# A two-layer hybrid decoder trunk: small products spread further, head norms by ln and exp, gate rows through DRAM, Strassen products summed by product

## The chip, the core and the metric

The kernel runs on one core of a Trainium2 chip. Its engines work side by side: PE (TensorE, matrix products), DVE (VectorE, elementwise), ACT (ScalarE, functions and copies), POOL (GpSimd) and SP (SyncE, which here only issues DMAs). The metric is the device time of one execution in microseconds, a median of several runs.

## The reference, cut to what matters

Two layers over 512 positions and 1024 channels, all in float32. Layer 0 mixes tokens by an RG-LRU, layer 1 by gated linear attention (GLA); each is followed by a gated FFN with 2816 hidden channels.

```python
for i in range(DEPTH):
    mod = (c_act @ ada_w[i] + ada_b[i])[:, None, :]
    sh_m, sc_m, gt_m, sh_f, sc_f, gt_f = jnp.split(mod, 6, axis=-1)
    h = rmsnorm(x, norm_g[i, 0]) * (1.0 + sc_m) + sh_m
    y = rglru_mixer(...) if i % 2 == 0 else gla_mixer(...)
    x = x + gt_m * rmsnorm(y, norm_g[i, 1])
    h = rmsnorm(x, norm_g[i, 2]) * (1.0 + sc_f) + sh_f
    y = conv_ffn(h, ...)          # (gelu(conv(h @ w_up)) * ...) @ w_down
    x = x + gt_f * rmsnorm(y, norm_g[i, 3])
# in gla_mixer, per head: log_alpha = log_sigmoid(z @ w_alpha + b) / 16, chunked attention, then
o = rmsnorm(o, norm_g)            # over the 256 channels of a head
return (o * silu(r)) @ w_out
```

## The kernel before, in words

Weights come in units of 128 x 1024 floats (`load_upto`). A unit lands in a `raw` tile, ACT copies it to a rounded high half in a `w` tile, DVE (or, for some, a DMA that accumulates on POOL's queue) makes the low half. A float32 product is three fast products: high by high, high by low, low by high (`mm3`, `down_t`). Every product goes through line 547, so that line is nearly all of PE.

Stages, in order: the norm of x and the first mixer's projections; its recurrence; its output projection (`mixer_out`, `sublayer_out`); the first FFN; GLA; its output; the second FFN; the last residual (`last_down`). An FFN alternates "up" steps (two projections of 24 products, conv, gelu, split) with Strassen steps of the down projection: of its 22 hidden tiles 18 go in groups of four or two tiles by seven block products (`SGROUPS`, `SPROD`, `strassen`), the last four plainly (`SLAST`, `down_t`). Each Strassen product is added from PSUM to one or two of eight output tiles `y` by DVE: 12 additions for each of two token halves per group.

`sublayer_out` computes the output's four token tiles. `down_pair` makes tiles 0 and 1, `residual` multiplies by the gate row, takes mean squares, the root (`rstd_col`, a power on POOL) and updates x (`xbuf`, resident); `turned` transposes the normed x (line 554) back to channels, and the next stage's first four projections run on token halves while tiles 2 and 3 are finished (`proj_halves`). The gate as a row on all partitions comes from `gate_rows`: ACT and DVE scale the identity by a column, and ones times that on PE gives the row.

In GLA the query and key projections came first, `z` gave the decays by a small product per head (96 rows), and then sixteen chunks of value and output-gate projections (`GLA_CHUNKS`) were interleaved with 36 small items (`diag`, seven `level`s and `inter` per head, `SPREAD` = 15). `attend` makes a head's output; its norm (`rstd_bcast`) was four column sums by ones, a power on POOL (line 475) and four broadcasts by the identity, each of them two instructions in float32, into the bank `nr`.

The order on each engine isn't the order of the code. `Sched` records all operations with a duration, then lists them: on PE and SP by recorded number, on the others by the length of what follows; an operation is placed when its inputs are ready by the planner's own clock and its buffers are free. Each engine then runs its list strictly in that order, so an operation that is later on the chip than planned holds all behind it. Slots: `g` (512 floats, general), `gh` (256), `w`, `raw`, `araw`, seven PSUM banks `mm` and one `nr`.

## Time and profile before

| | |
|---|---|
| median of the runs | 1154.21 us (1153.03 to 1156.69, 3 runs) |
| profiled execution, its own time | 1152.12 us |
| its span | 1150.3 us |
| PE busy | 1118.4 us, 97% |
| DVE, ACT, POOL busy | 84%, 58%, 11% |
| HBM read, mean rate | 219.39 MB, 193 GB/s |
| granted PE clock, mean | 0.997 |

The span is what the trace covers; the time has a little around it. "Busy" is the union of an engine's instructions. A gap in brackets after a row is the idle time ahead of it, and the name behind the arrow is what ended it. In names such as mm<-g,w the output stands left (mm and nr are PSUM banks) and the inputs right; a form 128x512 is partitions by elements.

### The profile page before, as it was taken

The numbers are of one execution on the slowest core, as the hardware profiler recorded it, in microseconds if no ns is written. First come the engines' busy times: TensorE is split into PE (matmuls) and PEld (weight loads), VectorE is DVE, ScalarE is ACT, GpSimd is POOL, SyncE is SP. The second block draws the span as 40 slices with busy tenths as digits, with TensorE's granted clock in tenths as the row PEclk, the third lists the DMA queues.
The fourth block names the chain that finished last, engine by engine and source line by source line (L and its number), as shares of the span: only waits on it lengthen the run. The fifth ranks groups of instructions, "written<-read, shape, count | busy, mean of one in ns | idle before, by whom it ended". The sixth has DMA issues, their size and how long they took to land.

```text
span 1150.3 us, 15016 instructions
## 1 busy us (share of the span) xinstructions
PE 1118.4 (97%) x5361; PEld 928.3 (81%) x5361; DVE 961.9 (84%) x1671; ACT 669.5 (58%) x1051; POOL 124.3 (11%) x148
## 2 busy tenths in 40 slices
PE   8999999999999999999999899999999999999996
PEld 6876778888888888777888788888888888888885
DVE  6989888987889989888878689967877887878986
ACT  5489957655455463466889436448656445453442
POOL 1000011011101101101201201011010101001001
PEclk9999999999999999999999999999999999999998
DMA  9889645789878988873564848624466665768531
GB/s 366 293 290 342 184 138 192 192 230 245 231 201 242 237 252 224 207 213 110 169 174 118 229 147 239 218 74 126 132 159 163 171 184 152 188 173 203 149 106 74
DMA packets 62397, 222.47 MB, mean 193 GB/s; under 512 B 6929, under 2 KB 7569, under 8 KB 62322
## 3 DMA queue, kind: packets, MB, share of 16 engines
q1 hardware_dynamic: 48642, 172.22, 43.4%
q0 software_dynamic: 13680, 49.29, 23.9%
q8 instruction: 42, 0.69, 0.2%
q14 instruction: 33, 0.27, 0.1%
HBM read 219.39 MB, written 2.10 MB: 193 GB/s over the span
## 4 chain that ended last, share of the span: by engine, by line
PE 65%; ACT 12%; DVE 10%; DMA 8%; issue 2%; POOL 1%; SPq 0%; DVEq 0%; ACTq 0%; POOLq 0%
PE mm L547 64%; DMA raw<-in_wall_dram 6%; ACT g L520 6%; DVE g L470 3%; ACT w L527 2%; ACT L520 2%; DVE w L470 2%; DVE g L484 1%; DMA araw<-in_adaT_dram 1%; DVE w L484 1%; ACT w L520 1%; DVE araw L484 1%; POOL sm L475 1%; PE nr L547 1%; ACT g L527 1%
## 5 line engine op out<-in xcount | busy, mean ns | idle before, releaser
L547 PE MATMUL mm<-g,w 128*128 128x512 f32 (+2 forms) x2758 | 614.3, 380 | 0.1
L547 PEld LDWEIGHTS mm<-g,w 128*128 128x128 f32 (+1 forms) x2758 | 501.4, 188 | 99.3 <-issue 1.4
L547 PE MATMUL mm<-w,g 128*128 128x512 f32 (+1 forms) x1428 | 332.8, 389 | 4.0 <-DVE g L470 3.8
L547 PEld LDWEIGHTS mm<-w,g 128*128 128x128 f32 x1428 | 264.9, 188 | 59.6 <-DVE g L470 5.0
L527 ACT CAST w<-raw 128x1024 fp32r<-128x1024 f32 x206 | 212.0, 1038 | 107.1 <-DMA raw<-in_wall_dram 93.4
L470 DVE TENSOR_TENSOR w<-raw,w 128x1024 fp32r<-128x1024 f32 x157 | 188.2, 1208 | 26.7 <-ACT w L527 26.3
L484 DVE SCALAR_TENSOR_TENSOR g<-mm,const,g 128x510 f32<-128x510 f32 (+3 forms) x199 | 146.6, 747 | 55.0 <-ACT g L520 46.0
L470 DVE TENSOR_TENSOR g<-g,g 128x256 f32<-128x256 f32 (+3 forms) x264 | 142.5, 568 | 34.0 <-ACT g L520 23.8
L470 DVE TENSOR_TENSOR g<-g,mm 128x512 f32<-128x512 f32 (+1 forms) x241 | 153.3, 681 | 15.1 <-PE mm L547 13.0
L520 ACT ACTIVATE g<-mm,const 128x512 f32<-128x512 f32 x115 | 86.8, 761 | 83.3 <-PE mm L547 81.1
L520 ACT ACTIVATE g<-g 128x512 f32<-128x512 f32 (+1 forms) x147 | 76.1, 549 | 82.7 <-DVE g L484 60.5
L562 POOL DMA_DIRECT2D w<-in_wall_dram x49 | 42.7, 871 | 506.3 <-ACT w L520 440.7
L484 DVE SCALAR_TENSOR_TENSOR araw<-araw,const 128x1024 f32<-128x1024 f32 x72 | 87.2, 1220 | 11.2 <-DMA araw<-in_adaT_dram 11.2
L547 PE MATMUL mm<-g,g 128*128 128x256 f32 (+3 forms) x508 | 78.4, 309 | 0.2 <-DVE g L470 0.2
L527 ACT CAST g<-g 128x512 fp32r<-128x512 f32 (+1 forms) x80 | 47.3, 602 | 53.2 <-DVE g L470 51.0
L547 PEld LDWEIGHTS mm<-g,g 128*128 128x128 f32 (+1 forms) x508 | 70.4, 191 | 5.7 <-DVE g L470 0.6
L520 ACT ACTIVATE w<-raw 128x1024 fp32r<-128x1024 f32 x49 | 51.8, 1058 | 39.7 <-DMA raw<-in_wall_dram 38.3
L475 POOL TENSOR_TENSOR sm<-sm,const 128x1 f32<-128x1 f32 (+2 forms) x34 | 35.9, 1057 | 283.4 <-DVE sm L484 191.7
L562 POOL DMA_DIRECT2D raw<-in_wall_dram x46 | 40.0, 870 | 208.9 <-DMA raw<-in_wall_dram 65.0
L520 ACT ACTIVATE g<-mm 128x512 f32<-128x512 f32 x44 | 25.9, 595 | 20.7 <-PE mm L547 11.0
L520 ACT ACT_TABLE_LOAD x24 | 30.8, 1283 | 1.1 <-PEq L1669 0.7
L484 DVE SCALAR_TENSOR_TENSOR w<-w,const 128x1024 f32<-128x1024 f32 x24 | 28.9, 1222 | 0.3 <-DMA w<-in_adaT_dram 0.3
(115 smaller groups left out, 716.4 us busy)
## 6 DMA issues: line engine op xcount, KB each, us to landing
raw<-in_wall_dram SPq DMA_DIRECT2D x218, 512.0 KB, 4.7
araw<-in_adaT_dram SPq DMA_DIRECT2D x72, 512.0 KB, 4.9
w<-in_wall_dram POOLq DMA_DIRECT2D x49, 512.0 KB, 8.5
raw<-in_wall_dram POOLq DMA_DIRECT2D x44, 512.0 KB, 7.2
w<-in_adaT_dram SPq DMA_DIRECT2D x24, 512.0 KB, 7.6
const<-in_xT_dram SPq DMA_DIRECT2D x4, 512.0 KB, 5.3
const<-in_x_dram SPq DMA_DIRECT2D x4, 512.0 KB, 10.7
out_dram<-const SPq DMA_DIRECT2D x8, 256.0 KB, 2.0
```

Of the source, the lines that this page charges most:

```text
L470: self.s.add(eng, dur, lambda: e.tensor_tensor(out.ap(), a.ap(), b.ap(), op=op), [a, b], [out])
L475: lambda: self.nc.gpsimd.tensor_tensor(out.ap(), a.ap(), b.ap(), op=ALU.pow), [a, b], [out])
L484: return self.nc.vector.scalar_tensor_tensor(out.ap(), a.ap(), f(sc), b.ap(), op0=op0, op1=op1, **kw)
L520: return self.nc.scalar.activation(out.ap(), a.ap(), func, **kw)
L527: self.s.add("act", (0.095 if self._sb(a) else 0.052) + out.n * 0.8325e-3, lambda: self.nc.scalar.copy(out.ap(), a.ap()), [a], [out], afte ...
L547: r.append(self.nc.tensor.matmul(g[0].ap(), g[1].ap(), g[2].ap(), start=g[3], stop=g[4], **kw))
L562: self.s.add("pool", 1.2, lambda: self.nc.gpsimd.dma_start(out.ap(), src, accum_op=ALU.add), [out], [out], xfer=nbytes / 180e3)
```

## The change

Six edits, with the planner's figures among them.

- GLA: the last five query and key projections become chunks; the 36 small items are spread over chunks 3 to 20 instead of 1 to 15. The last eight columns of the conditioning move into the second FFN.
- Head norm: one column sum onto all partitions by two fast products (`colsum`, after a cast on ACT and a subtraction on DVE), then Ln and Exp with scale -0.5 on ACT. `gated_to` follows when its output gate is there.
- Gate rows: PE transposes the eight columns, ACT copies them, SP stores them to DRAM and loads them back twice, broadcast to all partitions.
- Strassen: each of the seven products of a token half has an accumulator of its own; `outputs` makes the eight `y` tiles once at the end by 16 additions. Four of the seven live in `xbuf`, so x is stored to DRAM after each mixer and read back into `g` tiles (`old`) after the last up step.
- x's first load stands after the recurrence instead of after the first weights.
- Planner: a model of two DMA queues, durations of DVE and ACT times 1.04, a small random offset on priorities, one bank in reserve; slots g 43 to 42, gh 10 to 9, araw 2 to 3.

```diff
+SUMS = ("f0", "f1")
+SOUT = {7: (0, 0), 5: (0, 1), 2: (1, 0), 6: (1, 1)}
-GLA_CHUNKS = ([("v", t) for t in range(4)] + [("r", 0), ("r", 1), ("r", 2), ("r", 3), ("v", 4), ("v", 5),
-              ("v", 6), ("v", 7), ("r", 4), ("r", 5), ("r", 6), ("r", 7)])
-GLA_ENDS = (6, 9, 14, 16)
-SPREAD = 15
+GLA_CHUNKS = ([("q", n) for n in range(4, 9)] + [("v", t) for t in range(4)] + [("r", n) for n in range(4)] +
+              [("v", t) for t in range(4, 8)] + [("r", n) for n in range(4, 8)])
+GLA_ENDS = (11, 14, 18, 20)
+SPREAD = 2, 20
...
-DMA_LAT = 2.0
+DMA_LAT = 2.2
+DMA_HW, DMA_SW = (393e3, 132e3, 1.63, 1.11, 0.34), (220e3, 123.5e3, 1.74, 1.85, 0.0)
+SEEDS, NUDGE = (10, 10, 10, 10, 10, 10), 0.5
+MARGIN = {"dve": 1.04, "act": 1.04}
...
     def gate_rows(layer, part, late):
...
         rows = [gt(), gt()]
+        ps, cols, dr = mmtile(), gtn(P), s.buf("dram", F32, P, KD)
+        o = part * KD
+        s.add("pe", 0.112, lambda: nc.tensor.transpose(ps[0:P].rows(KD).ap(), mod[layer][o:o + KD].ap(), ident[:].ap()),
+              [mod[layer][o:o + KD], ident[:]], [ps[0:P]], after=late)
+        e.acopy(cols.rows(KD), ps[0:P].rows(KD))
+        e.store(dr[:], cols.rows(KD), KD * P * 4)
         for f in range(2):
-            hi, lo = gt(FR), gt(FR)
-            for k in range(4):
-                c = slice(k * P, (k + 1) * P)
-                e.act(hi[c], ident[:], AF.Copy, scale=mcol(layer, part, 4 * f + k), after=late)
-                e.stt(lo[c], ident[:], mcol(layer, part, 4 * f + k), hi[c].f32(), ALU.mult, ALU.subtract)
-            ps = mmtile()
-            e.mms([(ps[:], onesr[:], hi[:], True, False), (ps[:], onesr[:], lo[:], False, True)])
-            e.acopy(rows[f][:], ps[:])
+            e.load(rows[f][:], dr[:].map(lambda a, f=f: a.rearrange("k p -> (k p)")[f * S:(f + 1) * S]
+                                         .partition_broadcast(P)), P * S * 4)
...
-                e.stt(xr, yv, rp, xr, ALU.mult, ALU.add)
+                e.stt(xr, yv, rp, xo[t, f][:] if old else xr, ALU.mult, ALU.add)
...
+            if not old:
+                e.store(kept[t][:], xrows(t, 0, D), P * D * 4)
...
+            if sub in SUMS:
+                if (i, t) not in y:
+                    if i in SOUT:
+                        th, f = SOUT[i]
+                        y[i, t] = xrows(2 * th + t, f * S, (f + 1) * S)
+                    else:
+                        y[i, t] = gt()[:]
+                    e.acopy(y[i, t], ps[:])
+                else:
+                    e.tt(y[i, t], y[i, t], ps[:], ALU.add)
+                continue
...
+    def outputs(acc, y, th):
+        for t in range(2):
+            m = {i: acc[i, t] for i in SPROD}
+            for dst, src, op in (((7, 5, ALU.subtract), (7, 1, ALU.add), (7, 4, ALU.add), (5, 3, ALU.add)),
+                                 ((6, 2, ALU.subtract), (6, 1, ALU.add), (6, 3, ALU.add), (2, 4, ALU.add)))[th]:
+                e.tt(m[dst], m[dst], m[src], op)
+            for i in SOUT:
+                if SOUT[i][0] == th:
+                    y[2 * (2 * th + t) + SOUT[i][1]] = m[i]
...
-        rb = rstd_bcast(acc, S, 256, busy=1.5)
+        sums = s.buf("nr")
+        colsum(sums[:], acc[:])
         rs = gt()
-        e.acopy(rs[:], rb[:])
+        e.act(rs[:], sums[:], AF.Ln, bias=epsc[0:1], scale=1.0 / 256, table=("ln",))
+        e.act(rs[:], rs[:], AF.Exp, scale=-0.5, table=("exp",))
```

Three places show how instructions move. First PE in GLA, where the first small products stand. Before, 104 products lay between the four gate products (mm_5303 to mm_5313, output<-inputs) and the first level's two (gh, 128x256):

```order
L547 MATMUL mm_5313<-g_5143,g_5292 128x512
L547 MATMUL mm_5273<-g_4870,w_4901 128x512
...
L547 MATMUL mm_5521<-g_5258,const_93 128x512
L547 MATMUL mm_5521<-g_5271,const_93 128x512
L547 MATMUL mm_5524<-gh_5412,const_93 128x256
```

and of the change:

```order
L621 MATMUL mm_5244<-g_5118,g_5222 128x512
L621 MATMUL mm_5248<-g_4793,w_4963 128x512
...
L621 MATMUL mm_5339<-g_5188,const_88 128x512
L621 MATMUL mm_5339<-g_5202,const_88 128x512
L621 MATMUL mm_5345<-g_4793,w_5094 128x512
...
L621 MATMUL mm_5373<-gh_5355,const_88 128x256
```

Now 59 products lie between: two query or key projections, the diagonal's two and nine of the third.

Second, PE at the first head's norm (bank nr), which follows the head's output (the last row with gh, 128x128, is its end). Before:

```order
L547 MATMUL mm_5913<-g_5529,gh_5731 128x128
L547 MATMUL mm_5930<-g_4818,w_5696 128x512
...
L547 MATMUL mm_5930<-g_4831,w_5696 128x512
L547 MATMUL nr_5951<-const_82,g_5924 128x1 x4
L547 MATMUL mm_5930<-g_4840,w_5696 128x512
...
L547 MATMUL mm_5930<-g_4878,w_5696 128x512
L547 MATMUL nr_5951<-const_99,sm_5969 128x128 x4
```

and of the change:

```order
L621 MATMUL mm_5945<-g_5349,gh_5766 128x128
L621 MATMUL mm_5960<-g_4793,w_5725 128x512
...
L621 MATMUL mm_5960<-g_4862,w_5725 128x512
L621 MATMUL nr_5996<-g_5981,const_88 128x512
L621 MATMUL nr_5996<-g_5988,const_88 128x512
L621 MATMUL mm_5960<-g_4854,w_5725 128x512
```

Nine products of a gate projection stood between output and column sums, and 15 more before the broadcast; now 15 stand between, and nothing on PE reads the root.

Third, SP at the first FFN's output. Before, only weights and columns of the conditioning stood there:

```order
L557 DMA raw_4532<-in_wall_dram 128x128
L557 DMA raw_4591<-in_wall_dram 128x1024
L557 DMA raw_4603<-in_wall_dram 128x1024
L557 DMA raw_4608<-in_wall_dram 128x1024
L557 DMA araw_4639<-in_adaT_dram 128x1024
```

and of the change (g_4611 and g_4613 are the gate row's halves, the other g tiles old x):

```order
L632 DMA g_4566<-dram_1509 128x512
L642 DMA dram_4569<-gh_4564 8x128
L632 DMA g_4574<-dram_1509 128x512
L632 DMA g_4577<-dram_1736 128x512
L632 DMA g_4582<-dram_1736 128x512
L632 DMA g_4589<-dram_1757 128x512
L632 DMA g_4593<-dram_1757 128x512
L632 DMA g_4611<-dram_4569 128x512
L632 DMA g_4613<-dram_4569 128x512
L632 DMA raw_4620<-in_wall_dram 128x1024
```

Eight loads of old x (three of them ahead of the store), the store and the two loads of the row stand ahead of the next weight.

More of the change, by code (lines that the diff above doesn't have):

```diff
@@ L13 @@
 ALU = mybir.AluOpType
-PSUM = bass.MemoryType.PSUM
+PSUM, DRAM = bass.MemoryType.PSUM, bass.MemoryType.DRAM
 P = 128
@@ L948, in rstd_col, with sublayer_out @@
         return rp[0:1]
-    def sublayer_out(sub, src, y, gate, nexth):
+    xkept = {}
+    def sublayer_out(sub, src, y, gate, nexth, held=None, xo=None, old=None):
+        before = s.last["pe"]
         layer, gpart = gate
@@ L999, in turned @@
                     e.tt(hl[k][1][sl], hv, hl[k][0][sl].f32(), ALU.subtract)
+        if old:
+            for t in range(NT):
+                old(t)
+        if held:
+            held(0)
         for t, pss in enumerate(down_pair(sub, src, (0, 1))):
             residual(t, pss)
+        if held:
+            held(1)
         turned(0)
@@ L1012, in sublayer_out, with last_down @@
         return rest()
-    def last_down(hid, y, rows):
+    def last_down(hid, y, rows, xo, old):
+        for t in range(NT):
+            old(t)
         for t in range(NT):
@@ L1333, in trunk @@
             recur(range(2 * b - 2, 2 * b + 2))
+    for t in range(NT):
+        e.load(xbuf[t * D:(t + 1) * D], x_d[t], P * D * 4, s.last["pe"])
     for m in RGG[4]:
```

232 lines of the change are left out of this document (162 added, 70 removed).

## The prediction

> **What bounds the kernel now.** I read the page's first part, then busy time by stretch, then who waited for whom on PE, then the timeline at the longest of those waits.
>
> ```profile
> span 1150.3 us, 15016 instructions
> PE 1118.4 (97%) x5361; PEld 928.3 (81%) x5361; DVE 961.9 (84%) x1671; ACT 669.5 (58%) x1051; POOL 124.3 (11%) x148
> 0.00:29.00 29.00, 23.81 (x95) 18.82 (x96) 20.21 (x38) 15.13 (x28) 3.71 (x11) 1.00 0.94 365
> 600.00:700.00 100.00, 95.33 (x546) 81.66 (x545) 82.75 (x175) 62.41 (x119) 17.68 (x17) 1.00 0.57 155
> 1000.00:1100.00 100.00, 100.00 (x442) 82.80 (x442) 87.36 (x131) 47.28 (x60) 8.62 (x10) 1.00 0.67 175
> ```
>
> The last three rows are stretches: PE, PEld, DVE, ACT, POOL busy, granted clock, DMA share, GB/s. In the second FFN PE never stops and issues 442 products of 512 columns in 100 us: 0.226 us each. PE sets the end there, so only fewer products shorten it, and DVE at 87% is worth nothing by itself. PE is idle for 1150.3 - 1118.4 = 31.9 us:
>
> ```profile
> PE mm L547 <- DVE g L470: 3.9, 3, 2.4
> PE mm L554 <- ACT gh L520: 3.0, 3, 2.1
> PE nr L547 <- DVE g L470: 2.8, 1, 2.8
> PE mm L554 <- ACT g L520: 2.8, 5, 1.3
> PE nr L547 <- DVE gh L470: 2.7, 1, 2.7
> PE mm L547 <- DMA araw<-in_c_dram: 2.5, 1, 2.5
> PE nr L547 <- POOL sm L475: 1.9, 1, 1.9
> PE mm L547 <- ACT g L520: 1.7, 3, 1.3
> PE mm L547 <- DVE g L484: 0.2, 1, 0.2
> 1119.74 20.71 PE L547 MATMUL mm<-w,g 128*128 128x512 f32 x102
> ```
>
> The waits (total, times, longest) are 21.5 us, and 9.9 more follow the last product (1119.74 + 20.71 = 1140.45). No one wait is large. What the change can earn is fewer instructions on PE plus the waits that it touches.
>
> **The change, part by part.** *PE's own work.*
>
> ```profile
> 729.60 0.90 PE nr L547 x8
> 734.06 0.89 PE nr L547 x8
> 778.97 1.27 PE mm L554 x8
> L547 PE MATMUL mm<-g,const 128*128 128x512 f32 x24 | 8.4, 424 | 1.8 <-ACT g L520 1.5 <-DVE g L484 0.2
> L547 PE MATMUL nr<-const,g 128*128 128x1 f32 x32 | 4.1, 248 | 2.8 <-DVE g L470 2.8
> ```
>
> A head norm has eight column sums (32 over four heads, last row) and eight broadcasts: 0.90 + 0.89 = 1.79 us in the chain, 7.16 for four heads. Each becomes two products of 512 columns: 8 x 0.226 = 1.81. Of the 24 in the fourth row, 16 belong to the four calls of gate_rows (the other 8 to the diagonals, which stay): 16 x 0.226 = 3.62 go, four transposes at 1.27 / 8 = 0.16 come, 0.64. Net 7.16 - 1.81 + 3.62 - 0.64 = **8.3 us** that no order can give back. The FFNs' products keep their number.
>
> *The waits that it touches.*
>
> ```profile
> 482.79 1.88 DVE L470 TENSOR_TENSOR g<-g,mm 128x512 f32<-128x512 f32 x3 [0.24 <-PE mm L547]
> 484.13 0.96 PE L547 MATMUL mm<-w,g 128*128 128x512 f32 x3 [1.38 <-DVE g L470]
> 506.82 0.89 PE L547 MATMUL mm<-g,const 128*128 128x512 f32 x2 [1.33 <-ACT g L520]
> 645.14 1.06 ACT L520 ACTIVATE w<-raw 128x1024 fp32r<-128x1024 f32 x1 [5.15 <-DMA raw<-in_wall_dram]
> 649.52 1.05 PE L547 MATMUL nr<-const,g 128*128 128x1 f32 x8 [2.80 <-DVE g L470]
> 655.99 1.16 PE L547 MATMUL nr<-const,sm 128*128 128x128 f32 x8 [1.88 <-POOL sm L475]
> L470 DVE TENSOR_TENSOR g<-g,mm 128x512 f32<-128x512 f32 (+1 forms) x241 | 153.3, 681 | 15.1 <-PE mm L547 13.0
> ```
>
> Gate rows: PE's waits at 506.82 and two smaller ones at 143 us are the 1.5 + 0.2 that the x24 row carries, **1.7**. They end: the transpose reads finished columns. Head norm: POOL's power goes and PE waits for no root any more, **1.88**. The 2.80 ahead of it hangs on the sum of squares, whose squares stand on ACT behind a weight that landed 5.15 us late. The new chain is longer (a cast and a subtraction, 0.6 and 0.7 us) but PE now has 15 products of cover instead of 9, 6 x 0.226 = 1.4 us more. Ends 0 and 2.8; the three other heads show no such wait in the list, so I take **2.8**. First FFN's last group of two tiles: a Strassen product is three matmuls, 0.68 us, and up to two DVE additions, 1.25; PE waits 1.38 for a bank. With one addition per product (0.63) DVE keeps up; ends 0 and 1.4, I take **1.4**. Over both FFNs the additions from PSUM fall from 239 to 127 and 32 combinations come: 80 x 0.681 = 54 us less DVE, hidden behind PE everywhere else and so costed at nothing.
>
> *What it adds.*
>
> ```profile
> 579.10 1.21 PE L547 MATMUL mm<-g,g 96*128 96x512 f32 x4 [0.15 <-DVE g L470]
> 594.33 0.43 DVE L470 TENSOR_TENSOR gh<-gh,gh 128x256 fp32r<-128x256 f32 x1 [0.44 <-ACT gh L527]
> L520 ACT ACT_TABLE_LOAD x24 | 30.8, 1283 | 1.1 <-PEq L1669 0.7
> 581.17 1.28 ACT L520 ACT_TABLE_LOAD   x1
> 582.46 0.63 ACT L520 ACTIVATE g<-g 128x512 f32<-128x512 f32 x1
> ```
>
> Small products earlier: the first level's product now stands 59 products behind the four gate products, 1.21 + 59 x 0.226 = 14.5 us from their start; in this trace its operand was ready 594.76 - 579.10 = 15.7 us after it, though nothing hurried it. Exposed 0 to 1.2; I take **-1.2**. What waits behind it are the query and key products. Tables: 24 loads become 28, 4 x 1.283 = 5.1 us of ACT in a stage where it is 62% busy, plus eight Ln and Exp for four copies and four small DVE steps. PE reads none of these results before the mixer's output, so 0; with that cover gone -5.1. [...]
>
> DRAM:
>
> ```profile
> raw<-in_wall_dram SPq DMA_DIRECT2D x218, 512.0 KB, 4.7
> out_dram<-const SPq DMA_DIRECT2D x8, 256.0 KB, 2.0
> 520.30 17.22 PE L547 MATMUL mm<-w,g 128*128 128x512 f32 x75
> 530.05 0.68 DVE L470 TENSOR_TENSOR g<-g,g 128x512 f32<-128x512 f32 x1
> ```
>
> 36 transfers join SP's queue. The tight place is the first FFN's output: the rows are first used 530.05 - 520.30 = 9.8 us after the down products start. Now the copy on ACT (under 0.6), the store (2.0), five loads of old x ahead (256 KB at 365 GB/s, 0.7 each) and the rows' own load (at most 4.7) add to 0.6 + 2.0 + 3.5 + 4.7 = 10.8 at worst and 7.3 if the five run beside the store. Late by 0 to 1.0, and the next weights queue behind; I take **-0.5**. At the mixers' outputs 69 and 42 down products stand between the transpose and the first bank that meets a row, 15.6 and 9.5 us against 7.3 with nothing ahead, and in the second FFN many more: 0. The stores of x have no reader for an FFN long: 0, with the SP hold of rival 3 if their cover is gone. Moving x's first load off the stretch with DMA at 0.94 gains nothing, for no wait of PE names it.
>
> Sum: 8.3 + 1.7 + 1.9 + 2.8 + 1.4 - 1.2 - 0.5 = **14.4 us**. The profiled execution took 1152.12 us (span 1150.3), so 1137.7 by it; the median of the runs shown, 1154.21, is 2.1 above it, which gives **1139.8**. From the term bounds alone: at least 8.3 + 1.7 + 1.9 - 1.2 - 1.0 - 5.1 = 4.6, at most 16.1.
>
> **Rivals.** (1) *More waits close.* The planner's queue figures, margins and order change everywhere. The turns (PE mm L554: 3.0 + 2.8) and a split ahead of the first mixer's output (2.4) are planned waits too; if all close, 8.2 more: 1131.6. For it: DVE, on whose results the turns hang, is relieved. Against: those chains run through squares, POOL's root and a scaling that stay as they were. (2) *Only the instructions count*: every order has its own small waits, those that end reappear elsewhere, 1154.2 - 8.3 = 1145.9. For it: the waits come singly, from late weights, as at 645.14. (3) *Slower: SP held at the way through DRAM.* SP issues in order; while it waits for the store of a gate row before loading it back, no weight is issued: 2.0 + 4.7 = 6.7 us at each of three outputs, and a weight 5.15 us late cost PE 2.80 above. If nothing covers it, 20.1 - 14.4 = 5.7 over: 1159.9; it decides once a hold costs PE over 4.8 us. Against: eight w tiles of converted weights stand ahead of PE, and SP's order puts loads between store and read-back. (4) *The sums by product do nothing they should*: 14 first copies on ACT instead of 8, and 16 combinations pile up ahead of the down products; then the 1.4 is lost, 1141.2, inside the forecast.
>
> **How the numbers follow.** Forecast 0.55, (1) 0.18, (2) 0.20, (3) 0.07. The range runs from 1131, where (1) lies, to 1148, two us past (2); (3) and the tails, under 0.2, are left out. A change of under 0.3%, 3.5 us, can't be told from none: of (2) some 0.03 falls there, so faster 0.90, same 0.03, slower 0.07.
>
> **What would show it.** Right: PE's busy time lower by about 8; no wait of PE for POOL at nr in the second mixer; no PE wait for gate rows at the three outputs; DVE some 50 us less busy; the second FFN still at 442 products per 100 us; 28 table loads. Wrong: a wait of PE of over 2 us between the four gate products and the first level; at the first FFN's output a DVE row that waits for the load of a gate row; casts of weights on ACT that wait over 5 us for their load behind a read-back. The forecast falls if new waits of PE sum to over 6 us or the old ones shrink by 8.

## The result, and the profile after

| | before | after |
|---|---|---|
| median of four runs beside each other, us | 1155.45 (1153.03 to 1158.08) | 1129.39 (1127.77 to 1129.75) |
| ratio | | 0.9771, 95% interval 0.9746 to 0.9797 |
| profiled execution, us (span) | 1152.12 (1150.3) | 1129.75 (1128.0) |
| TensorE instructions | 5361 | 5293 |
| TensorE idle in the span, us | 31.9 | 22.5 |

The change saves 26.1 us by the medians and 22.4 by the profiled executions; forecast were 14.4. PE's busy time fell by 12.9 us, where the prediction's sign said about 8. First the page of the kernel after: span, busy times, ScalarE's table loads, and two stretches (columns as in the prediction: PE, PEld, DVE, ACT, POOL busy, granted clock, DMA share, GB/s).

```profile
span 1128.0 us, 14808 instructions
PE 1105.5 (98%) x5293; PEld 919.2 (81%) x5293; DVE 912.2 (81%) x1559; ACT 673.9 (60%) x1039; POOL 113.8 (10%) x144
L594 ACT ACT_TABLE_LOAD x28 | 35.9, 1283 | 3.5 <-PE nr L621 2.3
600.00:700.00 100.00, 100.00 (x545) 85.81 (x544) 87.63 (x182) 67.88 (x127) 10.66 (x14) 1.00 0.61 174
1000.00:1100.00 100.00, 100.00 (x443) 82.84 (x442) 82.35 (x117) 43.68 (x56) 6.04 (x7) 1.00 0.60 163
```

The second FFN issues 443 products in 100 us as before (442), VectorE is 49.7 us less busy, the loads of tables are 28: all as forecast. New is the stretch from 600 to 700 us, in mixer 2: PE is busy for all of it, where it had lost 4.7 us. Then the waits of PE (total, times, longest):

```profile
PE nr L621 <- DVE gh L544: 3.5, 1, 3.5
PE mm L621 <- DMA araw<-in_c_dram: 2.4, 1, 2.4
PE mm L628 <- ACT gh L594: 2.0, 3, 1.1
PE mm L628 <- ACT g L594: 1.5, 4, 0.6
PE mm L621 <- DVE sm L569: 1.1, 1, 1.1
PE mm L621 <- DVE g L544: 0.8, 1, 0.8
PE mm L621 <- DVE g L558: 0.7, 1, 0.7
PE mm L621 <- ACT g L601: 0.4, 1, 0.4
```

They add up to 12.4 us against 21.8. The first two lie in the first 10 us and were there before. Of the rest none is over 1.1 us. Gone are POOL, the sum of squares and the gate rows, which the forecast had named, and also the split wait of 2.4 us at 141 us and 2.3 of the 5.8 us at the turns, which it had left standing.

To see where each kernel loses time, I take the **lag** of PE: when an instruction starts, less the steady duration of all PE instructions issued ahead of it (0.227 us for 512 columns, 0.174 for 384, where the traces of before and after have 0.177, 0.120 for 256, about 0.11 for 128 and less, as the trace has them where they follow each other without a gap; the 192 narrower products of the levels, 0.06 to 0.11 in the trace, are rounded up, which takes some 2 us off mixer 2 in every row alike). The table gives the lag that each stage adds, in us: up to the first down product of mixer 1's output; that output up to its last turn; FFN 1 up to its output's first turn; from there to the gate products; mixer 2 up to its output's first turn; the rest up to the last product. The last column is the steady work. Every row is one profiled execution; those of b1, c2, d2 and d3 were the slowest of their kernels, 4 to 5 us above the medians.

| kernel | mixer 1 | its output | FFN 1 | its output | mixer 2 | rest | steady work |
|---|---|---|---|---|---|---|---|
| before | 23.4 | 7.4 | 4.6 | 2.7 | 7.6 | 0.7 | 1093.9 |
| after | 24.4 | 1.0 | 1.2 | 3.8 | 1.1 | 0.9 | 1085.5 |
| a1 old planner | 31.9 | 2.4 | 7.9 | 3.6 | 1.6 | 1.2 | 1085.5 |
| a3 no nudges | 29.9 | 0.7 | -0.1 | 4.0 | 0.7 | 1.5 | 1085.5 |
| a4 seed 11 | 38.1 | 1.2 | 1.7 | 5.7 | 0.3 | 1.0 | 1085.5 |
| d2 other draw | 24.2 | 2.5 | 5.0 | 3.2 | 0.8 | 1.0 | 1085.5 |
| d4 old buffer counts | 27.8 | 2.5 | 0.6 | 4.2 | 1.2 | 0.9 | 1085.5 |
| b1 power norm | 24.7 | 0.9 | 5.8 | 3.8 | 0.8 | 1.2 | 1090.7 |
| b2 late small products | 24.7 | 1.1 | 0.6 | 3.2 | 11.8 | 0.9 | 1085.5 |
| b3 old rows | 25.1 | 2.8 | 0.1 | 4.1 | 0.4 | 0.4 | 1088.7 |
| b4 direct sums | 24.2 | 1.1 | 5.2 | 7.8 | 3.6 | 0.3 | 1085.5 |
| d3 early x | 26.0 | 7.8 | 4.8 | 3.8 | 1.6 | 0.8 | 1085.5 |
| a2 before, new planner | 29.3 | 1.8 | 11.3 | 3.7 | 8.1 | 0.4 | 1093.9 |
| c1 = a2 + early small | 29.3 | 1.7 | 11.4 | 3.4 | 7.1 | 1.2 | 1093.9 |
| d1 = a2, another draw | 30.9 | 2.0 | 6.5 | 3.4 | 2.6 | 1.9 | 1093.9 |
| c2 before + ln/exp | 23.7 | 8.7 | 6.4 | 2.7 | 12.2 | 2.3 | 1088.7 |
| c3 before + rows | 23.6 | 7.7 | 1.0 | 7.3 | 3.9 | 0.9 | 1090.7 |
| c4 before + sums | 24.2 | 7.3 | 6.9 | 6.2 | 8.4 | 1.0 | 1093.9 |
| e1 before + late x | 25.0 | 9.1 | 6.2 | 3.2 | 9.5 | 1.8 | 1093.9 |
| e2 = e1 + sums | 22.9 | 8.6 | 8.5 | 6.3 | 6.1 | 3.8 | 1093.9 |

Before to after, the steady work falls by 8.4, mixer 1's output by 6.4, FFN 1 by 3.4 and mixer 2 by 6.5 us; 1.0 and 1.1 are lost in mixer 1 and at FFN 1's output. One of c2's ten executions took 6035.51 us and is left out of its median below.

### The profile page after: what moved, and what is told of

It is laid out like the page before. It is cut to its first block, busy times and chain, and to the rows that moved or that the text cites. A ratio compares the mean times of both kernels' runs of the same rounds, so it can differ in the third digit from the quotient of the medians.

```text
span 1128.0 us, 14808 instructions
## 1 busy us (share of the span) xinstructions
PE 1105.5 (98%) x5293; PEld 919.2 (81%) x5293; DVE 912.2 (81%) x1559; ACT 673.9 (60%) x1039; POOL 113.8 (10%) x144
## 4 chain that ended last, share of the span: by engine, by line
PE 72%; DMA 14%; DVE 5%; ACT 4%; issue 3%; POOL 0%; SPq 0%; DVEq 0%; POOLq 0%; ACTq 0%
PE mm L621 71%; DMA raw<-in_wall_dram 10%; DMA w<-in_adaT_dram 2%; DVE w L544 1%; ACT g L594 1%; ACT w L601 1%; DMA g<-dram 1%; DVE g L544 1%; DVE g L558 1%; PE mm L628 1%; DMA const<-in_par_dram 1%; DVE const L544 1%; PE nr L621 1%; ACT w L594 0%; DVE const L558 0%
## 5 line engine op out<-in xcount | busy, mean ns | idle before, releaser
L544 DVE TENSOR_TENSOR g<-g,g 128x256 f32<-128x256 f32 (+2 forms) x251 | 135.5, 564 | 32.6 <-ACT g L594 20.3
L594 ACT ACTIVATE g<-g 128x512 f32<-128x512 f32 (+1 forms) x136 | 68.9, 541 | 26.1 <-DVE g L558 19.8
L601 ACT CAST g<-g 128x512 fp32r<-128x512 f32 (+2 forms) x84 | 49.9, 605 | 50.7 <-DVE g L544 50.7
L544 DVE TENSOR_TENSOR const<-const,mm 128x512 f32<-128x512 f32 (+1 forms) x81 | 53.4, 676 | 7.0 <-PE mm L621 6.6
L549 POOL TENSOR_TENSOR sm<-sm,const 128x1 f32<-128x1 f32 (+1 forms) x30 | 25.5, 854 | 271.5 <-DVE sm L558 237.7
L594 ACT ACTIVATE g<-const 128x512 f32<-128x512 f32 x47 | 29.0, 630 | 33.3 <-DVE const L544 19.6
```

What stands on the lines that cost most here:

```text
L544: self.s.add(eng, dur, lambda: e.tensor_tensor(out.ap(), a.ap(), b.ap(), op=op), [a, b], [out])
L549: lambda: self.nc.gpsimd.tensor_tensor(out.ap(), a.ap(), b.ap(), op=ALU.pow), [a, b], [out])
L594: return self.nc.scalar.activation(out.ap(), a.ap(), func, **kw)
L601: self.s.add("act", (0.095 if self._sb(a) else 0.052) + out.n * 0.8325e-3, lambda: self.nc.scalar.copy(out.ap(), a.ap()), [a], [out], afte ...
```

## The experiments

All times are medians; the kernel before, run beside each, lay between 1154.2 and 1155.5 us. A ratio's interval is about 0.25% or 3 us wide to each side (less with more runs), so between two changed kernels a difference under some 4 us is not clear of noise.

### Is it the planner or the program? (a1 to a4)

a1 is the changed program with `Sched.order` and the costs of transfers of before; a2 the program of before with the change's:

```diff
-class Queues: ...            # a1; a2 has the opposite
-MARGIN = {"dve": 1.04, "act": 1.04}
+DMA_LAT, DMA_ISSUE = 2.0, 0.45
-SEEDS, NUDGE = (10, 10, 10, 10, 10, 10), 0.5
+SEEDS, NUDGE = (10, 10, 10, 10, 10, 10), 0.0   # a3
+SEEDS, NUDGE = (11, 11, 11, 11, 11, 11), 0.5   # a4
```

> The changed program, ordered by the planner of before: one common line of transfers in place of two queues, no 4% margin on VectorE and ScalarE times, no random nudges, TensorE taken as slow until 7 us instead of 20; buffers, products and norms stay those of the change. 1129.4 us is the changed kernel's median, and its TensorE idles some 14 us less between first and last matmul than before, of which the prediction had named 6 (three waits of 1.7, 1.9 and 2.8 us). Theory A, the planner's better figures closed the other 8 us: this kernel gives them back, 1136 to 1140 us, and the waits return where the edits did not touch the work, at the split ahead of mixer 1's output (2.4 us at 141 us) and at mixer 1's output turns (about 2 us). Theory B, the edits closed them by taking load off VectorE and ScalarE: 1128 to 1132 us, with no wait of 2 us between 100 and 1000 us. Theory C, any new order moves the time by some us either way: 1126 to 1136 with waits at places that neither theory names.

> The program of before with only the planner of the change (two transfer queues, 4% margin, a late slow start; its nudges are zero here, one product bank held in reserve as the change does, since otherwise the order does not close). Its instructions are those of before. Theory A: 8 us faster than before, 1146 to 1148 us, the split wait of 2.4 us at 141 us and the 2 us at mixer 1's output turns gone, the POOL power wait (1.9 us), the gate-row waits and the 16 gate-row products still there. Theory B: 1152 to 1157 us, as before. Theory C: anywhere from 1148 to 1160 us, with old waits closed and others opened.

The second text errs in one point: a2 ran with nudges of 0.5 us, one draw of seed 10 over the whole program.

> The changed kernel without the random nudges (the priorities of all engines but TensorE and SyncE shift by up to about half a us, at fixed seeds; here by nothing). Nothing else differs. If the nudges were part of what closed the waits (theory A in its narrow form) it is 2 to 5 us slower, 1131 to 1135 us, with new TensorE waits of 1 us or more between 100 and 1000 us; theory B has 1128 to 1131 us; theory C up to 3 us either way.

> The changed kernel with other random nudges of the same size. It measures what a mere re-ordering is worth: theories A and B have 1128 to 1132 us; theory C a difference of over 3 us to the changed kernel or to the one without nudges.

| | us | ratio to before, 95% |
|---|---|---|
| a1 | 1146.68 | 0.9928, 0.9900 to 0.9956 |
| a2 | 1161.27 | 1.0049, 1.0032 to 1.0067 |
| a3 | 1133.63 | 0.9815, 0.9783 to 0.9847 |
| a4 | 1144.66 | 0.9909, 0.9881 to 0.9937 |

a1 gains 7.5 us on the kernel before beside it: about the steady work of 8.4 and nothing more. Theory B falls, since the edits alone closed waits in some stages and opened as many in others; and theory A falls in its plain form, since the planner alone, with this draw, is slower. a2's loss is mostly one wait, 8.01 us for ScalarE ahead of the first turn of FFN 1's output (549.17 us), which another draw does not have (d1, below). a4 shows how large theory C is: nothing but other random nudges costs 15 us, nearly all in mixer 1 (38.1 us of lag against 24.4). No nudges cost 4 in the medians, in the same stage, but there the intervals overlap. There ScalarE is full in both kernels; first four stretches of the kernel after, then the same of a4:

```profile
104.00:112.00 8.00, 8.00 (x23) 3.98 (x22) 7.75 (x12) 7.93 (x13) 1.31 (x2) 1.00 0.79 171
112.00:118.00 6.00, 6.00 (x28) 4.98 (x27) 5.27 (x11) 5.97 (x8) 0.88 (x1) 1.00 0.96 277
118.00:126.00 8.00, 8.00 (x37) 6.62 (x36) 7.86 (x11) 7.95 (x13) 0.00 (x0) 1.00 1.03 354
126.00:130.00 4.00, 4.00 (x19) 3.31 (x18) 4.00 (x7) 3.96 (x5) 0.00 (x0) 1.00 1.03 414
```

```profile
104.00:112.00 8.00, 4.98 (x15) 2.45 (x13) 5.41 (x9) 7.91 (x11) 0.87 (x1) 1.00 0.91 263
112.00:118.00 6.00, 3.24 (x4) 0.91 (x4) 4.17 (x8) 5.94 (x8) 0.87 (x1) 0.60 1.03 317
118.00:126.00 8.00, 5.09 (x8) 2.74 (x9) 6.66 (x10) 7.71 (x14) 0.00 (x0) 0.50 1.04 351
126.00:130.00 4.00, 4.00 (x17) 3.22 (x17) 3.93 (x6) 3.94 (x4) 0.00 (x0) 0.90 1.03 419
```

PE gets through 107 products in 26 us with one order and 44 with the other, and from its first wait on the granted clock is down, 0.60 on average in the second stretch and 0.50 in the third. What it waited for (timeline of PE, the idle time and its releaser in brackets):

```profile
112.58 3.24 PE L621 MATMUL mm<-g,raw 128*128 128x512 f32 x4 [3.60 <-ACT g L594]
120.91 3.78 PE L621 MATMUL mm<-g,raw 128*128 128x512 f32 x4 [5.08 <-ACT g L594]
```

Operands that ScalarE makes, while ScalarE has hardly any idle time: it did something else first. Table loads of 1.28 us are part of it (four between 100 and 125 us in a4, five in a1, four in a3, two in the change), but before has four as well without these waits. This points to which of ScalarE's operations came first, and to the loads only in part; no run changes that alone.

### One part undone in the changed kernel (b1 to b4, d3, d4)

```diff
-        colsum(sums[:], acc[:])                       # b1
-        e.act(rs[:], sums[:], AF.Ln, ...); e.act(rs[:], rs[:], AF.Exp, scale=-0.5, ...)
+        rb = rstd_bcast(acc, S, 256, busy=1.5)
+        e.acopy(rs[:], rb[:])
-GLA_ENDS = (11, 14, 18, 20); SPREAD = 2, 20          # b2, with the q chunks ahead of the loop
+GLA_ENDS = (6, 9, 14, 16);   SPREAD = 0, 15
-    ps, cols, dr = mmtile(), gtn(P), s.buf("dram", F32, P, KD)   # b3: gate_rows of before
-SUMS = ("f0", "f1")                                  # b4, and x stays in xbuf
+SUMS = ()
```

> The changed kernel with one part undone: the head norms of mixer 2 again by column sums, a power on GpSimd, transposed copies and a broadcast, as before; everything ahead of mixer 2 is left as it was (its order differs little). By the prediction's sum: TensorE's own work grows by 5.35 us and the wait for GpSimd's power returns (1.88 us once), 1136.6 us; the lag that mixer 2 adds on TensorE, 7.6 us before and 1.1 us in the change, comes back by about 1.9 besides the work. Rival, the work only: 1134.7 us, since the small products that now start earlier give TensorE other work while the power runs. Rival, dearer: all four heads wait and the sum of squares is late again (2.8 us), 1139 us or more.

> The changed kernel with one part undone: all eight query and key projections first, then the value and gate projections with the small products between them, as before; the norms stay by ln and exp. By the prediction's sum 1.2 us faster to no change, since the first level's products stand behind more of other work: 1128 to 1130 us. Rival: the early start is what closed mixer 2's wait for a late sum of squares (2.8 us before, at 649 us) and its float32 stretches, so the lag that mixer 2 adds returns by 2 to 5 us: 1131.5 to 1135 us.

> The changed kernel with one part undone: the four pairs of gate rows by scaled identities (32 operations on ScalarE and 32 on VectorE in all) and a ones product, as before. By the prediction's sum: 2.98 us of TensorE's own work and waits of 1.7 us return, 1134 us. Rival: the rows' operations are what made VectorE and ScalarE late ahead of and in mixer 1's output, where the lag of TensorE grew by 7.4 us before and by 1.0 us now; then 4 to 6 us of lag return between 125 and 200 us besides the work: 1136 to 1139 us. Rival: a mere new order there, any sign, with the waits at 110 to 125 us that the kernels with other orders have.

> The changed kernel with one part undone: FFN products go straight into the eight output sums (an add or subtract for every use), x stays in its buffer, and no product sums, no kept copy of x and no reading back are there. By the prediction's sum the wait of 1.4 us near 484 us returns and 0.5 us of gain does too: 1130.3 to 1131.5 us, VectorE 50 us busier. Rival 4 of the prediction, the sums earn nothing: 1129 us or a little below, since the 1.1 us wait at 544 us, which is new, may go. Rival: the lag that FFN 1 adds (4.6 us before, 1.2 in the change) returns whole: 1132.8 us; FFN 2 stays without a wait.

d3 puts the loop that loads x back behind the first adaptive products; d4 takes the old line of buffer counts:

```diff
-    for t in range(NT): e.load(xbuf[...], x_d[t], P * D * 4, s.last["pe"])   # d3: ahead of RGG[4]
+    for t in range(NT): e.load(xbuf[...], x_d[t], P * D * 4)                 #     behind xps
-MMRES = 1; GEN, GH, ..., ARAW = 42, 9, ..., 3                                # d4
+MMRES = 0; GEN, GH, ..., ARAW = 43, 10, ..., 2
```

> The changed kernel with x (2 MB in four transfers) again loaded near the start instead of behind the last gate product's block of mixer 1. By the prediction, which gave this move nothing: 1129 to 1130 us. Rival: its 2 MB stand ahead of weights in the queue while mixer 1 has the most bytes to fetch, and a weight comes late: 3 to 7 us of lag between 100 and 200 us, 1132 to 1137 us, with TensorE waits on DMA or on casts that wait for it.

> The changed kernel with the buffer counts of before (43 general, 10 half-size, 2 of the adaptive raw ring, no product bank held in reserve) in place of 42, 9, 3 and 1. If buffers bound something: 1132 us or more, with a wait of over 1 us in FFN 1 or mixer 2 that the change lacks; if not, 1128 to 1131 us, within what a new order does.

Each of these kernels also gets a new order, with the seeds of the change. Since a new draw alone cost 15 us in a4, the differences below are not yet the worth of a part; what counts is whether the trace names the wait.

| undone | us | ratio to before, 95% | over the change, us | the prediction's term |
|---|---|---|---|---|
| b1 ln/exp norms | 1134.94 | 0.9824, 0.9802 to 0.9846 | 5.5 | 5.35 + 1.88 |
| b2 early small products | 1138.42 | 0.9857, 0.9835 to 0.9880 | 9.0 | -1.2 |
| b3 rows through DRAM | 1134.66 | 0.9826, 0.9804 to 0.9848 | 5.3 | 2.98 + 1.7 |
| b4 sums by product | 1140.28 | 0.9874, 0.9853 to 0.9894 | 10.9 | 1.4 - 0.5 |
| d3 late x | 1137.81 | 0.9843, 0.9818 to 0.9867 | 8.4 | 0 |
| d4 buffer counts | 1138.39 | 0.9849, 0.9825 to 0.9872 | 9.0 | none |

**b1**: the 5.5 us are about what the instructions of the norms are worth. Steady work grows by 5.2; mixer 2 adds 0.8 us of lag, and its list of PE waits has no line with POOL though the power is back:

```profile
PE nr L621 <- DVE gh L544: 3.2, 1, 3.2
PE mm L621 <- DMA w<-in_wall_dram: 2.6, 1, 2.6
PE mm L621 <- DMA araw<-in_c_dram: 2.5, 1, 2.5
PE mm L628 <- ACT gh L594: 2.3, 3, 1.4
PE mm L621 <- DVE g L544: 1.6, 1, 1.6
PE mm L621 <- DVE g L558: 1.6, 1, 1.6
PE mm L621 <- DVE sm L569: 1.1, 1, 1.1
PE mm L628 <- ACT g L594: 1.1, 3, 0.6
PE mm L621 <- ACT g L601: 0.4, 1, 0.4
PE mm L621 <- DVE w L544: 0.3, 1, 0.3
```

(The DMA wait of 2.6, at 401 us, stands in the slowest of its five runs, 1139.8 us; the median is 4.9 below.) So the forecast's pair "POOL's power goes, 1.88" hung the wait on the wrong part: it stays closed with the power back.

**b2**: the largest surprise. Mixer 2 adds 11.8 us instead of 1.1:

```profile
729.26 0.63 ACT L594 ACTIVATE g<-g 128x512 f32<-128x512 f32 x1
729.92 1.41 DVE L558 SCALAR_TENSOR_TENSOR g<-mm,const,g 128x512 f32<-128x512 f32 x2 [3.75 <-ACT g L594]
730.73 1.26 PE L621 MATMUL mm<-araw,w 128*128 128x512 f32 x3 [2.92 <-DVE g L558]
743.12 0.27 PE L1010 MATMUL mm<-const,const 128*8 128x128 f32 x1 [1.45 <-DVE g L558]
746.47 0.80 PE L621 MATMUL mm<-w,g 128*128 128x512 f32 x1 [2.38 <-ACT g L601]
```

The first two rows show what PE waits for at 730.73: the Exp of a head's norm, then VectorE's multiplication that reads the head's output from its PSUM bank. PE's next product reads none of that, so what it can be waiting for is the bank. Between the column sum and the Exp stand the Ln and a table load of 1.28 us; the wait at 743.12 is the same for the last head. There 9 products stand between column sum and wait; in the change 33 follow the last head's column sum (721.73) without a wait, and c2, below, has 6 and waits 2.13 us (763.43). So the chain of Ln and Exp, costed at nothing because PE reads none of its results, cost nothing where 33 products followed the column sum, and 1.45 and 2.13 us where 9 and 6 did.

The forecast looked only at the start of the stage (the first level behind fewer products), where nothing came: there is no wait of PE over 0.3 us between the gate products and the first level of the change. Over all kernels, mixer 2 adds 0.3 to 3.6 us with the small products early and 2.6 to 12.2 with them late; only c1 stands out, early and 7.1.

**b3** comes out near the forecast's number, 5.3 by the medians against 4.7, but not by its waits. Steady work grows by 3.2 us; the gate rows' products are back and PE waits for none of them (the last column is their idle time, 1.8 us in before):

```profile
L621 PE MATMUL mm<-g,const 128*128 128x512 f32 x24 | 7.0, 402 | 0.0
```

The 1.8 us more of lag in mixer 1's output come from a wait of 0.94 us for VectorE at 147.59 us and shorter ones.

**b4**: VectorE is 42 us busier, as it should be, and lag comes back at FFN 1 (4.0), its output (4.0) and mixer 2 (2.5). At FFN 1's output the turns wait, and the granted clock is 0.50 for 6.8 us from 552.73 on:

```profile
550.45 0.66 PE L628 MATMUL mm<-const,g 128*128 128x128 f32 x4 [1.89 <-ACT g L594]
551.67 0.44 PE L628 MATMUL mm<-const,g 128*128 128x128 f32 x2 [0.57 <-ACT g L594]
553.55 1.54 PE L628 MATMUL mm<-const,g 128*128 128x128 f32 x6 [1.44 <-ACT g L594]
```

**d3**: mixer 1's output adds 7.8 us again, and the longest waits are for a weight and for a cast of one. That cast, the second row, did not wait for a load: ScalarE stood idle 4.55 us until VectorE was done with a `w` tile.

```profile
130.22 0.97 PE L621 MATMUL mm<-g,w 128*128 128x512 f32 x3 [1.39 <-DMA w<-in_wall_dram]
157.68 2.19 ACT L601 CAST w<-raw 128x1024 fp32r<-128x1024 f32 x2 [4.55 <-DVE w L558]
158.78 0.73 PE L621 MATMUL mm<-w,g 128*128 128x512 f32 x2 [2.73 <-ACT w L601]
```

**d4**: 9.0 by the medians. The profiled run was its fastest (1134.57) and shows a 2.4 us wait in mixer 1 for ScalarE; whether the buffers bind or the order differs is not told apart.

### One part alone on the kernel before (c1 to c4, e1, e2)

The same edits the other way round. c1 stands on a2, with the change's planner; e1 and e2 also hold one product bank in reserve, which before does not.

> The kernel before with the change's planner (a2, whose random nudges were on after all, seed 10 in one draw over the whole program, other than its text says) and with one part more: query and key projections spread among the chunks, the small products from the third chunk on, gating done when its gate column is there. The norms stay by GpSimd's power. Up to mixer 2 it is a2 instruction for instruction. Compared with a2 (1161.3 us; mixer 2 adds 8.1 us of lag on TensorE there). If the early start is what closes mixer 2's waits: its lag falls to 1 to 3 us and the GpSimd wait (2.3 us) goes, 1154 to 1156 us. By the prediction's sum it costs 1.2 us: 1162.5 us. If ln and exp were needed for it too: the GpSimd wait stays and 1158 to 1160 us.

> The kernel before, its own planner, with one part of the change: the head norms by ln and exp on ScalarE after a column sum on TensorE. By the prediction's sum 5.35 us of TensorE's work and the GpSimd wait of 1.88 us go: 1147 us against 1154.4. Rival, from the kernel with late small products and ln/exp norms (its mixer 2 added 11.8 us of lag): the work goes, the GpSimd wait goes, but new waits of 2 us and more stand near the last head, since nothing is left to cover the end of mixer 2: 1149 to 1153 us.

> The kernel before, its own planner, with one part of the change: gate rows by a transpose and a pass through DRAM. By the prediction's sum 2.98 us of work and 1.7 us of waits: 1149.7 us. Rival: with 64 fewer operations on ScalarE and VectorE the split wait of 2.4 us at 141 us and the waits at mixer 1's output turns close too (lag there 7.4 us before, 1.0 in the change): 1145 to 1147 us. Rival: the order near 110 to 125 us changes for the worse and 2 to 6 us of ScalarE waits open there.

> The kernel before, its own planner, with one part of the change: FFN products summed by product and combined at the end, x kept in DRAM and read back for the FFN outputs (x is still loaded early). By the prediction's sum 1.4 us of waits near 484 us go and 0.5 us at FFN 1's output: 1152.5 us. Rival, from the kernel with direct sums (10.9 us slower than the change): the lag of FFN 1 (4.6 us), of its output (2.5) and part of mixer 2's (7.6) go with VectorE's 45 us: 1146 to 1149 us. Rival 4, nothing: 1154 to 1155 us.

> The kernel before, its own planner (one product bank in reserve, since its order does not close otherwise), with x loaded ahead of the last gate block of mixer 1 instead of near the start. If the 2 MB early in the queue are what makes mixer 1 late (d3: 8.4 us slower with x early), 1147 to 1150 us, the lag ahead of and in mixer 1's output down by 5 to 7 us. By the prediction, nothing: 1154 to 1156 us.

> e1 with the sums by product and x kept in DRAM as well (c4's edit, which alone was 4 us slower). If the two are worth what undoing them costs the change (8.4 and 10.9 us): 1136 to 1142 us. If the sums gain only under the change's planner: e1's time plus 2 to 5 us.

| alone | us | ratio to before, 95% |
|---|---|---|
| c1 a2 + early small products (a2: 1161.27) | 1160.11 | 1.0050, 1.0032 to 1.0068 |
| c2 ln/exp norms | 1152.87 | 0.9983, 0.9967 to 1.0000 |
| c3 rows through DRAM | 1146.84 | 0.9929, 0.9904 to 0.9955 |
| c4 sums by product, x in DRAM | 1159.21 | 1.0033, 1.0017 to 1.0049 |
| e1 late x | 1157.36 | 1.0026, 1.0008 to 1.0043 |
| e2 late x and sums | 1164.60 | 1.0097, 1.0062 to 1.0133 |

Only the rows gain clearly (8.7 us). That is the time of the rival in c3's text, but not its place: mixer 1's output adds 7.7 us as before (7.4), and what is saved lies in FFN 1 and mixer 2. The norms save 5.2 us of steady work and lose 4.6 in mixer 2 (12.2 against 7.6), in part at the bank waits told under b2; the sums and the late load, whose undoing costs the change 10.9 and 8.4 us, make the kernel before slower, and slower still together. In c4 PE waits 3.0 us at FFN 1's output where before has no wait. VectorE is then at the residual of the last token tiles, which now takes the sums from x's place (`const`) and the old x from a buffer (`g`); PE's row, then VectorE's:

```profile
559.52 2.43 PE L549 MATMUL mm<-g,g 128*128 128x256 f32 x10 [3.01 <-DVE g L472]
```

```profile
556.14 2.73 DVE L486 SCALAR_TENSOR_TENSOR const<-const,sm,g 128x512 f32<-128x512 f32 x4
```

Of the twelve kernels here that have the sums, eleven wait at this product, 0.8 to 3.7 us (d2 does not); of the eight without them d1 waits 0.2 us and the others not. It is the price of the sums at this place; the change pays 1.1.

c3 at the gate products, where some of its gain is lost again:

```profile
581.70 1.65 PE L547 MATMUL mm<-g,g 96*128 96x512 f32 x3 [4.67 <-DVE g L470]
```

And c1: the POOL wait, which a2 has too, is not closed by the early start; 2.26 us at 764 us.

```profile
764.35 1.16 PE L607 MATMUL nr<-const,sm 128*128 128x128 f32 x8 [2.26 <-POOL sm L535]
```

### How much is the draw? (d1, d2)

```diff
-SEEDS, NUDGE = (10, 10, 10, 10, 10, 10), 0.5
+SEEDS, NUDGE = (215, 215, 215, 215, 215, 215), 0.5   # d1, on a2
+SEEDS, NUDGE = (107, 306, 322, 318, 315, 311), 0.5   # d2, on the change
```

> The program of before with the change's planner, as a2, but with the best of 17 random draws by the planner's own reckoning of its order (nudges of seed 215 in place of 10). Instructions as before. If the order is what gave the change its gain, a good draw does the same here: 1140 to 1145 us, against 1161.3 for a2 and 1155 before. If the edits are needed to close the waits: 1149 to 1156 us, with the GpSimd wait and mixer 2's lag of about 8 us as they were, and what is gained stands ahead of mixer 1's output.

> The changed kernel with another draw for each of its six pieces (107, 306, 322, 318, 315, 311), chosen among 150 by the planner's own reckoning; nothing else differs. If that reckoning holds on the chip, 1126 to 1129 us, a little below the change; if 1129.4 was a lucky point of the chip's own, 1131 to 1136 us.

d1: 1151.70 us, ratio 0.9981 (0.9964 to 0.9998). d2: 1130.45 us, ratio 0.9792 (0.9765 to 0.9819), no different from the change within the intervals. A chosen draw takes 9.6 us off a2, and still leaves it 22 above the change under the same planner. Mixer 2 adds only 2.6 us in d1, where a2 adds 8.1 with the same instructions. So 1129 is not one lucky point, and no draw tried on the program of before comes near it, though a draw can close much of a stage's lag.

## Why the prediction was wrong in size

The sign and the steady work were right; the forecast, 1139.8, lay 10.4 us above the result, and the range ended 1.6 above it. The time is that of rival (1), more waits close (1131.6, given 0.18), though of the 8.2 us of waits that it named only 4.7 went.

The step that failed is the waits. The forecast held the split ahead of mixer 1's output and the turns for fixed, since their chains stay as they were, and hung every other wait on one operation. The forecast's own sign for this came: the old waits shrank by over 8 us (the listed ones from 21.8 to 12.4). In the runs a wait went or stayed with the order: the 2.4 us of the split went whole and 2.3 of the turns' 5.8, though no edit touches them, and three waits stay closed when the operation that was named comes back (b1, b3). Between the two profiled executions the 22.4 us are 8.4 of counted work, 9.4 of waits and some 4.6 that no term priced. Of these 4.6, about 1.3 are the last product ahead of each gap, which in both traces lasts 0.39 us with 512 columns where in the stream the next starts 0.227 behind it, and 0.27 to 0.28 against 0.11 to 0.12 with 256 and 128 (14 gaps in place of 22), and about 1 falls in the first 29 us; the rest was not traced.

- **PE's own work, 8.3**: right. Counted 8.4; b1 gives 5.2 of steady work for the norms (5.35 forecast), b3 gives 3.2 for the rows (2.98). With before's planner (a1) the whole program gains 7.5 us, about this term alone: that is the time of rival (2), "only the instructions count".
- **The base, "the median is 2.1 above it"**: mis-sized. The saving is 22.4 us between the two profiled executions but 26.1 between medians. Before's profiled run is the shortest of its four, the change's the longest of its four. Part of that goes with the clock: of 64 runs of before beside the experiments the ten with a mean granted clock of 0.996 and more average 1153.5 us, the 15 at 0.992 and less 1156.4, all 1155.0; the profiled one had 0.997, as all four of the change. So the runs with the clock of the profiled one lie some 1.5 us below the mean; that a wait costs more in the others, as one does in c2 (last section), is an estimate, for none of them has a trace. The other 2 us are the runs' spread.
- **Small products earlier, -1.2**: failed. In the change the first level starts 580.08 - 565.70 = 14.4 us behind the first gate product, as counted (14.5), but its operand is there by then. What the early start is good for lies at the end of the stage (b2), which the forecast did not price.
- **POOL, 1.88, sum of squares, 2.8, and gate rows, 1.7**: they went, but not for the reasons given. b1 keeps the power and has neither of the first two; c3 keeps the norms whole, with before's planner, and its list has neither; b3 keeps the old rows and PE does not wait for them. They were waits of an order, not of an operation, and that the three terms came out at their size is luck.
- **FFN 1's bank, 1.4**: more than half of the wait stayed in the change, at the same kind of addition:

```profile
471.13 1.20 PE L621 MATMUL mm<-w,g 128*128 128x512 f32 x4 [0.79 <-DVE g L544]
```

  In b1 and d3 it is 1.6 us, with the sums. The 3.4 us that the stage's lag lost (4.6 to 1.2) are for the larger part the gate row's wait of 1.33 at 506.82 and the first turn's. Over all kernels FFN 1 adds -0.1 to 8.5 us with the sums and 1.0 to 11.4 without, so b4's 4.0 there can't be told from an order's. Rival 4 is thus not settled: the sums cost 10.9 us when undone in the change and 3.7 when added to before.
- **x's load, "gains nothing, for no wait of PE names it"**: not shown either way. d3 is 8.4 us slower, but its longest wait is for a `w` tile and not for a load. In the other kernels x's place does not go with the lag: a2, c1 and d1 load x early and add 1.7 to 2.0 us at mixer 1's output, e1 and e2 load it late and add 9.1 and 8.6.
- **DRAM, -0.5**: the sign that the forecast gave for this came, at the first FFN's output a VectorE row that waits for the load of a gate row:

```profile
520.36 0.69 DVE L544 TENSOR_TENSOR const<-const,g 128x512 f32<-128x512 f32 x1 [1.54 <-DMA g<-dram]
```

  The load landed at 520.27, 10.9 us after PE's transpose of the columns (509.36); the forecast's worst case was 10.8. At PE it shows as little: the first turn waits 0.35 us. FFN 1's output adds 1.1 us more lag than before because of another wait, 1.10 us at 544.69, for VectorE at the residual of the last token tiles. Of rival (3), SP issues nothing from 505.3 to 510.5 us, until the columns are copied, and no wait of PE for a weight follows.
- **Turns**: 5.8 us became 3.5.

What made the rest? By stages, the lag of mixer 1's output (7.4 to 1.0) goes with the planner: with the change's planner twelve of thirteen kernels add 0.7 to 2.8 us there, with before's six of seven 7.3 to 9.1 (d3 and a1 are the others). Mixer 2 (7.6 to 1.1) goes with the early small products (b2). FFN 1 goes with neither; there the draw is as large as the difference.

As whole kernels: before 1154 to 1155; only the planner 1161 and, with a chosen draw, 1152; only the program 1147; both 1129, and 1130 to 1145 with other draws or none. Chosen draw against chosen draw (d1, d2) the program is worth some 21 us under the change's planner, of which 8.4 are counted work; under before's planner it was worth 7.5, in the one order that was run. Undone singly, six parts cost 5 to 11 us each, 48 together, nearly twice the gain; alone on before (c1 on a2), five of them gain some 5 us together. So the time is not a sum over the edits. That an edit's room on VectorE or ScalarE becomes time only when the order is made for it fits these figures but was not shown: each removal also makes an order that was never chosen for that program, and a new order alone can cost 15 us. What of the planner does it, the two queues, the margin of 4% or the nudges, was not tried apart, and stays open, as does d4's loss.

## What to carry to other kernels

Price the instructions of the engine that is never idle: the counted work came in every pair of runs, though new waits can take it back (c2). Do not pin the small waits of a planned order on one operation. Before believing what a part is worth, undone or added, ask what a mere new draw of the order costs: here up to 15 us, more than any part. Where a stage ends in dependent chains, ask for each chain how many independent products are left behind it, and what it holds meanwhile: in b2 PE waited 2.92 us at 730.73, by my reading for a bank, although it reads no result of the chain.

## What the runs showed of the hardware

A PE wait of 2.40 us cost c2 1.8 us more than it lasted; in before nearly the same wait left the clock at 1.00. Before and c2 have the same instructions up to mixer 2, and both wait 2.4 us for the split at 141 to 143 us. Stretches of before, then of c2:

```profile
136.54:139.95 3.41, 2.36 (x11) 1.63 (x9) 2.79 (x4) 3.38 (x6) 0.00 (x0) 1.00 0.50 156
139.95:143.37 3.42, 2.07 (x8) 1.43 (x8) 3.26 (x5) 3.42 (x8) 0.00 (x0) 1.00 0.40 149
```

```profile
139.55:142.96 3.41, 1.02 (x5) 0.52 (x3) 2.73 (x4) 3.38 (x6) 0.00 (x0) 1.00 0.60 207
142.96:146.38 3.42, 3.41 (x8) 2.74 (x9) 3.31 (x8) 3.42 (x11) 0.00 (x0) 0.50 0.20 37
```

In c2 the granted clock is 0.50 for 3.4 us after the wait: 8 products in the stretch, each some 0.43 us apart instead of 0.227, and the lag grows by 1.8 us from the wait's end (142.97) to 149.96. In before it stays at 1.00.

The traces show where the two differ. c2 has five such stretches ahead of its last product, from 142.96, 511.60, 654.96, 726.63 and 764.18 us on, 3.4 us each, and the later four begin 108, 150, 171 and 182 times 3.413 us behind the first. In c1 the slow stretches begin 121 and 187 times 3.413 us behind the first (127.08, 540.12 and 765.36 us), in a1 84 times (117.48 and 404.22). So I count off windows of 3.413 us from a slow stretch of the same trace; in before and the change, which have none between 35 us and the last product, from the one behind that product (1143.47 and 1120.46 us).

In the windows that end at 580.56 us in c3, 559.62 in c4, 113.18 in a4, 142.96 in c2, 552.73 in b4 and 404.22 in a1, PE was idle for 3.41, 3.01, 2.81, 2.39, 2.33 and 2.04 us, and the clock in the next was 0.50. Before has no window of more than 1.82 us idle between 35 us and its last product, the change none of more than 1.32, and their clock stayed at 1.00; the windows in which the last product ends, with 3.02 and 2.37, were followed by 0.50. In these windows the clock thus went with the idle time within one of them and not with the length of a wait: before's longest after 35 us, 2.80 us up to 649.52, lies in two windows (1.82 and 0.98). The four rows above are windows too: c2's wait lies in one (3.41 - 1.02 = 2.39 us idle), before's is cut by an edge into 1.05 and 1.35. How much idle time it takes was not settled.

In a1 two waits, of 1.51 us and of 0.53, lie in the window that ends at 404.22:

```profile
402.35 0.73 PE L561 MATMUL mm<-w,gh 128*128 128x512 f32 x2 [1.51 <-ACT w L541]
405.00:408.00 3.00, 3.00 (x9) 2.37 (x8) 2.99 (x7) 2.67 (x5) 0.51 (x1) 0.56 0.80 208
```

From 35 us to its last product, the change has no wait over 1.1 us, its clock never leaves 1.00 there, and its four runs lie within 2 us; before's lie within some 5.
